# Gate tiles, activation buffers and accumulators in the expert stage of a hybrid decoder layer

## The chip, the cores and the metric

The kernel runs on one core of one Trainium2 chip. The metric is the time of one execution on the device in microseconds (us), taken as the median of several executions. TensorE is called PE here (PEld is its weight load), VectorE DVE, ScalarE ACT, GpSimd POOL, SyncE SP.

## The reference

One decoder layer over 1024 tokens (plus 16 meta tokens): a mixer (latent attention and retention, merged by gates), then a mixture of 16384 single-neuron experts. The change concerns the second part:

```python
def peer_sublayer(h, g_ffn, w_peer_q, keys_1, keys_2, peer_u, peer_v):
    x = rmsnorm(h, g_ffn).reshape(-1, shape[-1])
    q = (x @ w_peer_q).reshape(T, PEER_HEADS, PEER_DQ)
    ...
    eidx = (e1 * PEER_NKEYS + e2).reshape(T, PEER_HEADS * PEER_TOPK)
    gates = jax.nn.softmax(sc, axis=-1)
    ...
    def block(args):
        xt, it, gt = args
        act = jax.nn.gelu(jnp.einsum('td,tkd->tk', xt, peer_u[it]), approximate=False)
        return jnp.einsum('tk,tkd->td', gt * act, peer_v[it])
```

Each token has 128 chosen experts (8 heads of 16). For each it needs the dot product with a row of `peer_u`, a Gelu, the gate, and a weighted sum of rows of `peer_v`.

## The kernel before

The tokens are 8 blocks of 128. Three of them (group 0) take the **gathered** way: for each of the 128 chosen experts POOL fetches the 128 rows (one a token, 512 KB) by an indirect DMA, and DVE multiplies and sums (`gathered`, lines 1060 to 1091): first 128 steps with rows of `peer_u` against the normed tokens `xn`, then 128 steps with rows of `peer_v` added into two accumulators `acc`. At the start of a block `xn` and `acc[0]` are loaded and `acc[1]` is cleared; at its end the two are added and stored.

The other five blocks (640 tokens) take the **dense** way (`dense`, from line 1127): all 16384 experts are computed for all tokens, and a gate matrix that is zero for experts not chosen picks out what counts. The experts are 128 tiles of 128. Three steps belong to a tile: its scores (`scores`, line 1149: 48 matmuls into the buffers `tr`, then a Gelu by ACT into a tile `gl`), its weights (`weights`, line 1204: `gl` times the gates `gt` by DVE, then a split into `c_hi` by ACT and `c_lo` by DVE), and its part of the output (line 1239: matmuls of `c_hi` and `c_lo` with `peer_vt` into `zacc`). All products are made from a high and a low part of both factors in three matmuls (`mm3`, lines 246 to 248).

The dense part has two stages. In the **U stage** the scores of the first 48 tiles (AHEAD) are computed and stored to `gl_d`; meanwhile the routing of the last blocks and then the gate matrix (`gate_matrix`, 80 steps, stored to `gate_d` in 20 pieces) are made in the background. In the **V stage** the 128 tiles are taken in 16 groups of 8. The list `es` mixes quads of four stored tiles (their `gl` is loaded from `gl_d`, written L here) with quads of four tiles whose scores are computed now (C): the groups are CL, CL, CC, LC, and so on four times. In a group first come scores, loads and weights of its 8 tiles, then two passes (one for each half of the 1024 columns) of four pieces of `peer_vt` over 8 tiles, and after each pass five additions of `zacc` into `y` by DVE (line 1242). One gate tile `gt` holds the gates of four tiles, so each quad needs one; it is loaded in `weights` at a quad's first tile, into one buffer (GTB is 1). `gl` has three buffers, `c_hi` and `c_lo` eight, `raw` (a loaded piece of weights) three and its split parts three.

What sets the order around the change is a pacing by costs. Each piece that is split (`split_piece`, line 221) calls `pace` with `pacing["piece"]`, which is 6.5 in the dense part. `pace` gives each of two background queues that cost times a rate from RATES, and runs steps of the queue while its credit is positive: queue 0 the routing and gates (a gate step costs 1.7), queue 1 the gathered blocks (a row step costs 1.2). RATES[4] holds for the gate matrix, RATES[5] for the V stage. The rows of each engine are then put in order by the scheduler of the language, except for the row steps, which stay in the order of the program; SP issues all loads and stores but the gathered rows, in one queue.

Of the kernel before, what the change touches and what calls it, by code (L numbers as in the profile page):

```python
# [12 lines left out]
F32 = mybir.dt.float32  # L13
BF16 = mybir.dt.bfloat16
# [25 lines left out]
GE = 8  # L40
CB = 8
AHEAD = 48
RING = 3
ROWS = 4
SPLIT = 3
GTB = 1
DELAY = 8.0
# [3 lines left out]
LEAVE = ((6, 6, 3), (0, 1, 1))  # L51
RATES = ((0.0, 0.0), (0.5, 0.2), (0.3, 0.3), (0.8, 0.2), (0.8, 0.45), (0.0, 0.5))

# [90 lines left out]
def hybrid_layer(ctx: ExitStack, tc: tile.TileContext, out, a, dbg=None):  # L144
# [8 lines left out]
    dram = ctx.enter_context(tc.tile_pool(name="dram", bufs=1, space=DRAM))  # L153

    gat = ctx.enter_context(tc.tile_pool(name="gat", bufs=1, side="right"))

# [93 lines left out]
    def square_sum(src, acc):  # L250
        junk = work.tile([P, TW], F32, name="zt").bitcast(BF16)
        S.activation(junk[:, :src.shape[-1]], src, AF.Square, accum_out=acc)
# [63 lines left out]
    def group(g):  # L316
# [273 lines left out]
        def retention(hp):  # L590
# [45 lines left out]
            def add_state(i):  # L636
                pst = tr()
                for s in range(2):
                    T.matmul(pst[64 * s:64 * s + 64, 0:P], qn[:, i, 128 + 64 * s:128 + 64 * s + 64],
                             vr[:, i, P * s:P * s + P], start=True, stop=True)  # L640
                new = work.tile([P, P], F32, name=f"state{hp}")
                if hp in state:
                    V.tensor_tensor(new, pst[:, 0:P], state[hp], OP.add)
                else:
                    V.tensor_copy(new, pst[:, 0:P])
                state[hp] = new
# [179 lines left out]
        def merge():  # L826
            mg = own.mg
            for c in range(KD):
                for s, src in enumerate((own.oTs, own.yTs)):
# [6 lines left out]
                    for j, w in enumerate(split_pieces(a["w_ret" if s else "w_mla"][c], n, P)):  # L836
                        mm3(pz[:, 1, :W], w, src[j], j == 0, j == n - 1)
                        if j % 2:
                            yield
                    th = work.tile([P, TW], F32, name="zt")[:, :W]  # L840
                    S.activation(th, pz[:, 0, :W], AF.Tanh, scale=0.5)
# [218 lines left out]
    def gathered(b, eidx, gate):  # L1060
# [11 lines left out]
        nc.sync.dma_start(xn, xn_d[b])  # L1072
        acc = [gat.tile([P, D], F32, name=f"acc{s}", bufs=1) for s in range(2)]
        nc.sync.dma_start(acc[0], h2_d[b])
        V.memset(acc[1], 0.0)
        dots = work.tile([P, 128], F32, name="dots")
        for n in range(256):
            while todo and len(rows) < ROWS - 1:
# [4 lines left out]
            else:  # L1083
                if not k:
                    S.activation(dots, dots, AF.Gelu)
                    V.tensor_tensor(dots, dots, gate, OP.mult)
                op = V.scalar_tensor_tensor(acc[k % 2], row, dots[:, k:k + 1], acc[k % 2], op0=OP.mult, op1=OP.add)  # L1087
            tc.keep_in_program_order(op)
# [4 lines left out]

    def gate_matrix(i, kt, gT, p):

# [31 lines left out]
    def dense(xT):  # L1127
# [21 lines left out]
        def scores(e):  # L1149
            hi, lo = split_piece(1024, lambda r: nc.sync.dma_start(r, a["peer_ut"][e].rearrange("p c e -> p (c e)")))  # L1150
            gl = up.tile([P, DT], F32, name="gl", bufs=3)
            for n in order:
# [8 lines left out]
        def routes():  # L1161
# [12 lines left out]
            pacing["rates"] = RATES[4]  # L1174
            gms, gm = open_pool("gm")
            for i, (kt, gT) in enumerate(routed):
                yield from gate_matrix(i, kt, gT, gm)
            gms.close()
# [13 lines left out]
        for b in range(NGATH, NBLK):  # L1192
            ys.append(vp.tile([P, D], F32, name=f"y{b}"))
            nc.sync.dma_start(ys[-1], h2_d[b])
        gt = {}

        def activations(e):
            if e >= AHEAD:
                return scores(e)
            gl = up.tile([P, DT], F32, name="gl", bufs=3)  # L1200
            nc.sync.dma_start(gl, gl_d[e])
            return gl

        def weights(e, gl):

            if e % 4 == 0:
                gt[0] = vp.tile([P, nt, 4, TS], F32, name="gt", bufs=GTB)
                nc.sync.dma_start(gt[0], gate_d[:, :, TS * e:TS * e + 4 * TS].rearrange("n p (e t) -> p n e t", e=4))
            V.tensor_tensor(gl.rearrange("p (n t) -> p n t", t=TS), gt[0][:, :, e % 4],
                            gl.rearrange("p (n t) -> p n t", t=TS), OP.mult)  # L1210
# [5 lines left out]

        es = [4 * n + k for n in sorted(range(P // 4), key=lambda n: (n + 0.5) / AHEAD if 4 * n < AHEAD else
                                        (n + 0.5 - AHEAD / 4) / (P - AHEAD)) for k in range(4)]
        for e0 in range(0, P, GE):
            group = es[e0:e0 + GE]  # L1220
# [38 lines left out]
    V.tensor_scalar(g_gnh, g_gn, 0.5, None, op0=OP.mult)  # L1259
    mask_a = load_const("mask_a", a["c_mask_a"], [P, P])  # L1260
    mask_b, ident_b = (const.tile([P, P], BF16, name=n) for n in ("mask_b", "ident_b"))
    V.tensor_copy(mask_b, mask_a)
    V.tensor_copy(ident_b, ident)
    mask_r = load_const("mask_r", a["c_mask_r"], [P, P])
    iota = load_const("iota", a["c_iota"], [P, P])
    iota_i = const.tile([P, 16, 2 * H], BF16, name="iota_i")
    V.tensor_copy(iota_i, iota[:, 0:16].unsqueeze(2).to_broadcast([P, 16, 2 * H]))
    iota_2 = const.tile([P, P, 2], BF16, name="iota_2")
    V.tensor_copy(iota_2, iota.unsqueeze(2).to_broadcast([P, P, 2]))
    gqr = load_const("gqr", bcast(a["g_qk"], 32, 64), [P, 32])  # L1270
# [18 lines left out]
    for n, now in enumerate(groups):  # L1289
# [5 lines left out]
        interleave([now.merge()] + ([following.latents()] if following else []), STEPS[1][n])  # L1295
        rest = now.output()
    dense(rest)
    finish(1)

# [17 lines left out]
```

## Time and profile before

| what | us |
| --- | --- |
| median of three runs | 3574.49 (3563.3 to 3585.4) |
| the profiled execution | 3571.28 |
| its span, first to last instruction | 3569.5 |
| mixer and routing of the last group, about | 0 to 1420 |
| U stage, about | 1420 to 2003 |
| V stage, about | 2003 to 3560 |

The profile is of one execution. The profiled execution is within 0.1% of the median of the runs. Its span is 1.8 us shorter than its time. Busy times of PE overlap from one matmul to the next, so the step from one start to the next tells what a matmul takes, not its own duration.

### The profile page before, as it was taken

What the parts mean: (1) busy time and instruction counts of PE and PEld (TensorE: products, weight loads), DVE (VectorE), ACT (ScalarE), POOL (GpSimd) and SP (SyncE); (2) the same over time, 40 slices, a digit from 0 to 9 for tenths busy, and PEclk for the clock granted to TensorE, in tenths of its full rate; (3) what the DMA queues carried; (4) which work ended last, traced back from release to release, by engine and by line L of the source; (5) the groups of instructions that cost most, each with busy time, mean ns of one, the idle gap of its engine ahead of it and who ended that gap; (6) DMA issues with size and microseconds to landing.
All of it is one profiled execution on the core that took longest, in us unless ns stands there. A gap on an engine that the chain in (4) does not pass through costs nothing.

```text
span 3569.5 us, 53608 instructions
## 1 busy us (share of the span) xinstructions
PE 3322.8 (93%) x20376; PEld 3022.3 (85%) x20376; DVE 2687.7 (75%) x5659; ACT 1268.1 (36%) x2097; POOL 1090.4 (31%) x772
## 2 busy tenths in 40 slices
PE   8999989989789998999999799999999999999999
PEld 7888988788767898999999788888788778887788
DVE  5645469898796676798988578777778777877776
ACT  3445334544445533234566222222222222222221
POOL 0000000112011122013434445454445454554454
PEclk9999999999899999999999899999999999999999
DMA  3322353557654377456777888888889888988886
GB/s 129 121 78 94 133 193 113 167 201 253 215 156 139 135 239 254 152 177 238 284 289 295 305 289 305 306 308 301 287 284 321 288 291 290 322 307 288 286 300 246
DMA packets 329251, 837.12 MB, mean 235 GB/s; under 512 B 45713, under 2 KB 140689, under 8 KB 326177
## 3 DMA queue, kind: packets, MB, share of 16 engines
q1 hardware_dynamic: 218400, 431.00, 35.4%
q0 software_dynamic: 110592, 402.70, 32.0%
q8 instruction: 160, 2.62, 0.3%
q14 instruction: 99, 0.80, 0.1%
HBM read 755.16 MB, written 78.43 MB: 234 GB/s over the span
## 4 chain that ended last, share of the span: by engine, by line
PE 49%; issue 17%; DMA 13%; DVE 11%; POOL 6%; ACT 3%; POOLq 0%; SPq 0%; DVEq 0%; ACTq 0%
PE zacc L246 10%; PE zacc L248 10%; PE zacc L247 10%; DMA row<-in_peer_v_dram,eidx 7%; POOL row L1065 6%; PE tr L246 4%; PE tr L247 4%; PE tr L248 4%; DMA gt<-gate_d 3%; DVE wlo L219 2%; PE tr L765 2%; PE sc L729 1%; DVE acc L1087 1%; ACT whi L218 1%; DMA row<-in_peer_u_dram,eidx 1%
## 5 line engine op out<-in xcount | busy, mean ns | idle before, releaser
L1065 POOL DMA_INDIRECT row<-in_peer_u_dram,eidx x384 | 486.3, 1266 | 1731.5 <-DVE row L1082 839.9
L218 ACT ACTIVATE whi<-raw 128x1024 fp32r<-128x1024 f32 (+2 forms) x508 | 520.7, 1026 | 1274.3 <-PE zacc L248 643.5
L219 DVE TENSOR_TENSOR wlo<-raw,whi 128x1024 fp32r<-128x1024 f32 (+2 forms) x508 | 599.5, 1181 | 369.6 <-ACT whi L218 368.7
L1065 POOL DMA_INDIRECT row<-in_peer_v_dram,eidx x384 | 603.9, 1573 | 718.5 <-DVE acc L1087 605.4
L246 PE MATMUL zacc<-whi,c_hi 128*128 128x512 f32 x1280 | 509.1, 398 | 57.0 <-ACT c_hi L218 45.9
L1087 DVE SCALAR_TENSOR_TENSOR acc<-row,dots,acc 128x1024 f32<-128x1024 f32 x384 | 482.0, 1278 | 91.0 <-DMA row<-in_peer_v_dram,eidx 90.2
L248 PE MATMUL zacc<-whi,c_lo 128*128 128x512 f32 x1280 | 506.8, 396 | 2.9 <-DVE c_lo L219 2.9
L247 PE MATMUL zacc<-wlo,c_hi 128*128 128x512 f32 x1280 | 506.3, 396 | 0.0
L1082 DVE SCALAR_TENSOR_TENSOR row<-row,xn 128x1024 f32<-128x1024 f32 x384 | 463.2, 1218 | 54.7 <-DMA row<-in_peer_u_dram,eidx 54.3
L246 PE MATMUL tr<-xT_hi,whi 128*128 128x384 f32 (+1 forms) x1216 | 416.3, 342 | 40.5 <-ACT gl L1158 39.3
L247 PE MATMUL tr<-xT_lo,whi 128*128 128x384 f32 (+1 forms) x1216 | 411.9, 339 | 0.0
L248 PE MATMUL tr<-xT_hi,wlo 128*128 128x384 f32 (+1 forms) x1216 | 411.7, 339 | 0.0
L246 PEld LDWEIGHTS zacc<-whi,c_hi 128*128 128x128 f32 x1280 | 245.4, 192 | 115.2 <-ACT c_hi L218 49.3
L246 PE MATMUL tr<-x_hi,whi 128*128 128x256 f32 x1024 | 295.9, 289 | 12.7 <-ACT whi L218 10.2
L248 PEld LDWEIGHTS zacc<-whi,c_lo 128*128 128x128 f32 x1280 | 244.7, 191 | 60.0 <-DVE c_lo L219 8.6
L247 PE MATMUL tr<-x_lo,whi 128*128 128x256 f32 x1024 | 290.2, 283 | 0.0
L248 PE MATMUL tr<-x_hi,wlo 128*128 128x256 f32 x1024 | 290.1, 283 | 0.0
L247 PEld LDWEIGHTS zacc<-wlo,c_hi 128*128 128x128 f32 x1280 | 245.3, 192 | 50.7
L246 PEld LDWEIGHTS tr<-xT_hi,whi 128*128 128x128 f32 x1216 | 233.6, 192 | 43.2 <-ACT gl L1158 40.8
L246 PE MATMUL zacc<-whi,hn_hi 128*128 128x256 f32 x832 | 250.8, 301 | 3.8 <-ACT pT L780 1.3
L247 PE MATMUL zacc<-wlo,hn_hi 128*128 128x256 f32 x832 | 238.9, 287 | 1.4 <-DVE wlo L219 1.4
L248 PE MATMUL zacc<-whi,hn_lo 128*128 128x256 f32 x832 | 238.1, 286 | 0.0
(286 smaller groups left out, 6728.8 us busy)
## 6 DMA issues: line engine op xcount, KB each, us to landing
raw<-in_peer_ut_dram SPq DMA_DIRECT2D x128, 512.0 KB, 5.5
raw<-in_peer_vt_dram SPq DMA_DIRECT2D x128, 512.0 KB, 6.2
gate_d<-stage SPq DMA_DIRECT2D x20, 2048.0 KB, 9.1
gt<-gate_d SPq DMA_DIRECT2D x32, 1280.0 KB, 14.6
raw<-in_w_nat_dram SPq DMA_DIRECT2D x72, 512.0 KB, 3.5
raw<-in_w_z_dram SPq DMA_DIRECT2D x48, 512.0 KB, 3.3
gl_d<-gl SPq DMA_DIRECT2D x48, 320.0 KB, 2.9
gl<-gl_d SPq DMA_DIRECT2D x48, 320.0 KB, 6.4
```

The lines of the kernel that those rows point to most:

```text
L218: S.activation(hi, src, AF.Copy)
L219: V.tensor_tensor(lo, src, hi.bitcast(F32), OP.subtract)
L246: T.matmul(o, st[0], mv[0], start=first, stop=False)
L247: T.matmul(o, st[0], mv[1], start=False, stop=False)
L248: T.matmul(o, st[1], mv[0], start=False, stop=last)
L729: T.matmul(sc[:, c, 0:w], qh, kT[0:96, k0:k0 + w], start=True, stop=c < nch - 1)
L765: T.matmul(oo, vh[:, c + k], pT[:, k], start=False, stop=c + k == b)
L1065: G.indirect_dma_start(out=row, out_offset=None, in_=table, in_offset=bass.IndirectOffsetOnAxis(ap=eidx[:, k:k + 1], axis=0))
L1082: op = V.scalar_tensor_tensor(row, row, 1.0, xn, op0=OP.mult, op1=OP.mult, accum_out=dots[:, k:k + 1])
L1087: op = V.scalar_tensor_tensor(acc[k % 2], row, dots[:, k:k + 1], acc[k % 2], op0=OP.mult, op1=OP.add)
```

## The change

`gt` gets two buffers, and the tile of the next quad is loaded where the quad before it begins (the first before the first group). `gl` gets five buffers. RATES[4] goes from 0.8 to 0.9 for the gates, RATES[5] from 0.5 to 0.52 for the gathered rows. A gathered block waits for 6.0 of credit before its first row step. The second accumulator is no longer a buffer of its own: it takes the buffer of `xn` after the last step that reads `xn`, and its first step multiplies and does not add, so nothing is cleared. To make room, buffers that only the mixer needs (`zt`, the retention states, two masks and a bf16 identity) move to a pool `mw` that is closed before the dense part, and `iota_2` is made in the U stage, ahead of the gates.

```diff
+GLB = 5
-GTB = 1
+GTB = 2
-RATES = ((0.0, 0.0), (0.5, 0.2), (0.3, 0.3), (0.8, 0.2), (0.8, 0.45), (0.0, 0.5))
+RATES = ((0.0, 0.0), (0.5, 0.2), (0.3, 0.3), (0.8, 0.2), (0.9, 0.45), (0.0, 0.52))
...
+    mixers = ExitStack()
+    mw = mixers.enter_context(tc.tile_pool(name="mw", bufs=2))
...
-        junk = work.tile([P, TW], F32, name="zt").bitcast(BF16)
+        junk = mw.tile([P, TW], F32, name="zt").bitcast(BF16)
...
-                new = work.tile([P, P], F32, name=f"state{hp}")
+                new = mw.tile([P, P], F32, name=f"state{hp}")
...
-        acc = [gat.tile([P, D], F32, name=f"acc{s}", bufs=1) for s in range(2)]
+        acc = [gat.tile([P, D], F32, name="acc", bufs=1)]
         nc.sync.dma_start(acc[0], h2_d[b])
-        V.memset(acc[1], 0.0)
         dots = work.tile([P, 128], F32, name="dots")
+        yield 6.0
...
-                op = V.scalar_tensor_tensor(acc[k % 2], row, dots[:, k:k + 1], acc[k % 2], op0=OP.mult, op1=OP.add)
+                if k == 1:
+                    acc.append(gat.tile([P, D], F32, name="xn", bufs=1))
+                    op = V.tensor_scalar(acc[1], row, dots[:, k:k + 1], None, op0=OP.mult)
+                else:
+                    op = V.scalar_tensor_tensor(acc[k % 2], row, dots[:, k:k + 1], acc[k % 2], op0=OP.mult, op1=OP.add)
...
-            gl = up.tile([P, DT], F32, name="gl", bufs=3)
+            gl = up.tile([P, DT], F32, name="gl", bufs=GLB)
...
+            iota_2 = gm.tile([P, P, 2], BF16, name="iota_2")
+            V.tensor_copy(iota_2, iota.unsqueeze(2).to_broadcast([P, P, 2]))
...
-        gt = {}
+        gts = deque()
+
+        def gate_tile(e):
+            gts.append(vp.tile([P, nt, 4, TS], F32, name="gt", bufs=GTB))
+            nc.sync.dma_start(gts[-1], gate_d[:, :, TS * e:TS * e + 4 * TS].rearrange("n p (e t) -> p n e t", e=4))
...
             if e % 4 == 0:
-                gt[0] = vp.tile([P, nt, 4, TS], F32, name="gt", bufs=GTB)
-                nc.sync.dma_start(gt[0], gate_d[:, :, TS * e:TS * e + 4 * TS].rearrange("n p (e t) -> p n e t", e=4))
-            V.tensor_tensor(gl.rearrange("p (n t) -> p n t", t=TS), gt[0][:, :, e % 4],
+                if e != es[0]:
+                    gts.popleft()
+                if e != es[-4]:
+                    gate_tile(es[es.index(e) + 4])
+            V.tensor_tensor(gl.rearrange("p (n t) -> p n t", t=TS), gts[0][:, :, e % 4],
...
+        gate_tile(es[0])
         for e0 in range(0, P, GE):
...
+    mixers.close()
     dense(rest)
```

**SP at the start of the V stage.** In the rows below `y` is the output, `gt` a gate tile, `gl<-gl_d` the load of a stored tile's scores, `raw<-in_peer_ut_dram` a piece for scores and `raw<-in_peer_vt_dram` one for the output. Before:

```order
L1194 DMA y_21061<-h_d 128x1024
L1208 DMA gt<-gate_d 128x20x128
L1232 DMA raw<-in_peer_vt_dram 128x1024 x4
L1201 DMA gl<-gl_d 128x640 x2
L1232 DMA raw<-in_peer_vt_dram 128x1024
L1208 DMA gt<-gate_d 128x20x128
L1201 DMA gl<-gl_d 128x640
L1232 DMA raw<-in_peer_vt_dram 128x1024
L1201 DMA gl<-gl_d 128x640
L1232 DMA raw<-in_peer_vt_dram 128x1024
L1208 DMA gt<-gate_d 128x20x128
```

and now:

```order
L1208 DMA gt<-gate_d 128x20x128
L1194 DMA gl_d<-gl 128x640
L1157 DMA raw<-in_peer_ut_dram 128x1024
L1208 DMA gt<-gate_d 128x20x128
L1157 DMA raw<-in_peer_ut_dram 128x1024
L1194 DMA gl_d<-gl 128x640
L1157 DMA raw<-in_peer_ut_dram 128x1024
L1248 DMA raw<-in_peer_vt_dram 128x1024
L1194 DMA gl_d<-gl 128x640
L1248 DMA raw<-in_peer_vt_dram 128x1024 x4
L1214 DMA gl<-gl_d 128x640 x4
L1208 DMA gt<-gate_d 128x20x128 x2
```

The second `gt` used to stand behind the pieces of the first group's output and its first two stored tiles; now it stands three rows behind the first, ahead of two pieces for the last computed scores of the first group, and the two `gt` of the second group are together, ahead of three pieces of the first group's second pass. The stored tiles are loaded four at a time.

**DVE in the second half of a CL group.** This is the fifth group, from the last computed tiles of the C quad (`gl<-gt` is the multiplication by the gates, `c_lo` and `wlo` are low parts, `row,dots<-row,xn` a row step of a gathered block). Before:

```order
L1209 TENSOR_TENSOR gl<-gt,gl 128x640
L1082 SCALAR_TENSOR_TENSOR row,dots<-row,xn 128x1024
L219 TENSOR_TENSOR c_lo<-gl,c_hi 128x640
L1082 SCALAR_TENSOR_TENSOR row,dots<-row,xn 128x1024
L219 TENSOR_TENSOR wlo<-raw,whi 128x1024
L1082 SCALAR_TENSOR_TENSOR row,dots<-row,xn 128x1024
L1209 TENSOR_TENSOR gl<-gt,gl 128x640 x3
L219 TENSOR_TENSOR c_lo<-gl,c_hi 128x640 x3
L1082 SCALAR_TENSOR_TENSOR row,dots<-row,xn 128x1024 x2
L1209 TENSOR_TENSOR gl<-gt,gl 128x640
L219 TENSOR_TENSOR wlo<-raw,whi 128x1024
L219 TENSOR_TENSOR c_lo<-gl,c_hi 128x640
```

and now:

```order
L1224 TENSOR_TENSOR gl<-gt,gl 128x640
L1085 SCALAR_TENSOR_TENSOR row,dots<-row,xn 128x1024
L222 TENSOR_TENSOR c_lo<-gl,c_hi 128x640
L1085 SCALAR_TENSOR_TENSOR row,dots<-row,xn 128x1024 x2
L1224 TENSOR_TENSOR gl<-gt,gl 128x640 x5
L222 TENSOR_TENSOR c_lo<-gl,c_hi 128x640 x5
L222 TENSOR_TENSOR wlo<-raw,whi 128x1024
L1085 SCALAR_TENSOR_TENSOR row,dots<-row,xn 128x1024 x3
L222 TENSOR_TENSOR wlo<-raw,whi 128x1024
```

Before, the four stored tiles were multiplied in two goes (three and one), behind the split of the next `peer_vt` piece (`wlo`). Now the multiplications of the last computed tile and of all four stored tiles stand together, with their five `c_lo` behind them, and the split of the piece comes after these ten rows.

## Rows read from the trace of the kernel before

**Rows 1.** The page, part 1: busy time, share of the span, instructions.

```profile
PE 3322.8 (93%) x20376; PEld 3022.3 (85%) x20376; DVE 2687.7 (75%) x5659; ACT 1268.1 (36%) x2097; POOL 1090.4 (31%) x772
```

**Rows 2.** Windows: stretch, length, busy PE, PEld, DVE, ACT, POOL, clock, DMA, GB/s.

```profile
1700.00:1900.00 200.00, 200.00 (x1508) 199.59 (x1508) 178.52 (x198) 121.32 (x142) 91.91 (x38) 1.00 0.78 291
...
2003.00:3560.00 1557.00, 1455.55 (x7549) 1286.18 (x7548) 1191.90 (x1435) 362.60 (x491) 757.96 (x551) 0.96 0.85 295
2300.00:2400.00 100.00, 100.00 (x525) 88.46 (x524) 80.78 (x120) 21.65 (x28) 51.88 (x41) 1.00 0.91 318
...
2700.00:2800.00 100.00, 99.94 (x547) 89.80 (x546) 82.23 (x81) 23.54 (x32) 51.01 (x40) 1.00 0.89 314
3100.00:3200.00 100.00, 100.00 (x555) 90.44 (x555) 81.28 (x118) 25.32 (x37) 52.92 (x41) 1.00 0.87 301
```

**Rows 3.** Waits, 2003 to 3560: engine and line, releaser, us, times, longest.

```profile
DVE gl L1209 <- DMA gt<-gate_d: 107.4, 17, 9.5
DVE acc L1087 <- DMA row<-in_peer_v_dram,eidx: 66.9, 40, 5.7
...
PE zacc L246 <- ACT c_hi L218: 45.9, 8, 7.6
...
PE tr L246 <- ACT gl L1158: 41.4, 6, 20.1
...
PE zacc L246 <- DVE y L1242: 9.9, 10, 2.1
```

**Rows 4.** Timeline of three engines around one late gate tile (fifth group).

```profile
2426.08 0.37 SPq L1208 DMA_DIRECT2D gt<-gate_d  x1
...
2441.66 2.30 DVE L1209 TENSOR_TENSOR gl<-gt,gl 128x640 f32<-128x640 f32 x3 [8.19 <-DMA gt<-gate_d]
...
2443.31 0.79 PE L246 MATMUL zacc<-whi,c_hi 128*128 128x512 f32 x1 [6.53 <-ACT c_hi L218]
```

**Rows 5.** DMA issues by name: KB each, median us from issue to landing.

```profile
gt<-gate_d SPq DMA_DIRECT2D x32, 1280.0 KB, 14.6
...
xn<-xn_d SPq DMA_DIRECT2D x3, 512.0 KB, 4.4
```

**Rows 6.** Matmuls by line, 2003 to 3560: count, busy, mean ns, idle before.

```profile
L246 PE MATMUL zacc<-whi,c_hi 128*128 128x512 f32 x1276 | 507.5, 398 | 57.0 <-ACT c_hi L218 45.9 <-DVE y L1242 9.9 <-ACT whi L218 1.2
...
L246 PE MATMUL tr<-xT_hi,whi 128*128 128x384 f32 x624 | 215.5, 345 | 39.1 <-ACT gl L1158 39.0
...
L246 PE MATMUL tr<-x_hi,whi 128*128 128x256 f32 x617 | 174.3, 282 | 2.6 <-ACT gl L1158 2.4
```

**Rows 7.** Timeline of PE, 2003 to 2041: start, duration, instruction.

```profile
2003.00 0.28 PE L248 MATMUL tr<-x_hi,wlo 128*128 128x256 f32 x1
2023.34 0.69 PE L246 MATMUL tr<-xT_hi,whi 128*128 128x384 f32 x1 [20.06 <-ACT gl L1158]
...
2024.46 0.52 PE L246 MATMUL tr<-xT_hi,whi 128*128 128x384 f32 x1
2024.78 0.52 PE L247 MATMUL tr<-xT_lo,whi 128*128 128x384 f32 x1
...
2029.61 0.28 PE L246 MATMUL tr<-x_hi,whi 128*128 128x256 f32 x1
...
2032.46 0.34 PE L246 MATMUL tr<-xT_hi,whi 128*128 128x384 f32 x1
...
2036.63 0.39 PE L246 MATMUL zacc<-whi,c_hi 128*128 128x512 f32 x1
...
2040.52 0.39 PE L248 MATMUL zacc<-whi,c_lo 128*128 128x512 f32 x1
```

**Rows 8.** Groups by line, 1700 to 1900: the gate steps on DVE and PE.

```profile
L1120 DVE TENSOR_TENSOR ob<-eq,gT 128x1024 f32<-128x1024 bf16 x48 | 58.4, 1218 | 1.2 <-PE zacc L1105 1.2
L219 DVE TENSOR_TENSOR wlo<-raw,whi 128x1024 fp32r<-128x1024 f32 x17 | 20.8, 1224 | 19.8 <-ACT whi L218 19.8
...
L1105 PE MATMUL zacc<-ob,oa 128*128 128x128 f32 x754 | 95.5, 281 | 0.0
```

**Rows 9.** Waits of the SP queue for gate tiles, 2003 to 3560.

```profile
SPq L1208 <- DVE gl L1209: 50.4, 31, 5.5
```

More of the change, by code (lines that the diff above doesn't have):

```diff
@@ L839, in merge @@
                             yield
-                    th = work.tile([P, TW], F32, name="zt")[:, :W]
+                    th = mw.tile([P, TW], F32, name="zt")[:, :W]
                     S.activation(th, pz[:, 0, :W], AF.Tanh, scale=0.5)
@@ L1091, in gathered, with gate_matrix @@
         nc.sync.dma_start(out[P * b:P * b + P], acc[0])
-    def gate_matrix(i, kt, gT, p):
+    def gate_matrix(i, kt, gT, iota_2, p):
         stage = {}
@@ L1175, in routes @@
             gms, gm = open_pool("gm")
+            iota_2 = gm.tile([P, P, 2], BF16, name="iota_2")
+            V.tensor_copy(iota_2, iota.unsqueeze(2).to_broadcast([P, P, 2]))
             for i, (kt, gT) in enumerate(routed):
-                yield from gate_matrix(i, kt, gT, gm)
+                yield from gate_matrix(i, kt, gT, iota_2, gm)
             gms.close()
@@ L1199, in activations @@
                 return scores(e)
-            gl = up.tile([P, DT], F32, name="gl", bufs=3)
+            gl = up.tile([P, DT], F32, name="gl", bufs=GLB)
             nc.sync.dma_start(gl, gl_d[e])
@@ L1259, in hybrid_layer @@
     V.tensor_scalar(g_gnh, g_gn, 0.5, None, op0=OP.mult)
-    mask_a = load_const("mask_a", a["c_mask_a"], [P, P])
-    mask_b, ident_b = (const.tile([P, P], BF16, name=n) for n in ("mask_b", "ident_b"))
+    mask_a, mask_r = (mw.tile([P, P], F32, name=n, bufs=1) for n in ("mask_a", "mask_r"))
+    nc.sync.dma_start(mask_a, a["c_mask_a"])
+    mask_b, ident_b = (mw.tile([P, P], BF16, name=n, bufs=1) for n in ("mask_b", "ident_b"))
     V.tensor_copy(mask_b, mask_a)
     V.tensor_copy(ident_b, ident)
-    mask_r = load_const("mask_r", a["c_mask_r"], [P, P])
+    nc.sync.dma_start(mask_r, a["c_mask_r"])
     iota = load_const("iota", a["c_iota"], [P, P])
@@ L1267, in hybrid_layer @@
     V.tensor_copy(iota_i, iota[:, 0:16].unsqueeze(2).to_broadcast([P, 16, 2 * H]))
-    iota_2 = const.tile([P, P, 2], BF16, name="iota_2")
-    V.tensor_copy(iota_2, iota.unsqueeze(2).to_broadcast([P, P, 2]))
     gqr = load_const("gqr", bcast(a["g_qk"], 32, 64), [P, 32])
```

## The prediction

> **What bounds the kernel now.** I read the page first, then the windows by stage, then the waits of the V stage, then the timeline around one wait. The page says that PE is busy for 93% of the span [rows 1], so whatever gives time must do it where PE stands still or runs slowly. The windows show where: from 1700 to 1900, in the U stage, PE is busy for all 200 us at a granted clock of 1.00; from 2003 to 3560, in the V stage, it is busy for 1455.55 of 1557 us, at a clock of 0.96 [rows 2]. So 101.5 us are idle there.
>
> The waits name the reasons [rows 3]: PE waits 45.9 us in 8 goes for `c_hi`, 41.4 us in 6 goes for the Gelu's buffers `gl`, and 9.9 us for the additions into `y`. The first two are not the last link. DVE itself waits 107.4 us in 17 goes for `gt`, and one case shows the chain [rows 4]: the load of `gt` is issued at 2426.08, DVE gets it at 2441.66 (8.19 us idle), and PE begins again at 2443.31 after 6.53 us. A load takes 14.6 us to land [rows 5], and with one buffer it can't be issued before the last tile of the quad before has been multiplied. The 8 waits for `c_hi` are as many as there are CL groups (8 of 16): there the stored quad comes second, and PE has no scores to do meanwhile. The waits for `gl` belong to the first group (20.06 us [rows 7]) and to four CC groups, where the computed tiles run out of their three buffers behind a DVE that stands; a sixth of 2.4 us is of the other segment [rows 6] and not clearly of this kind.
>
> An idle stretch costs more than itself. After the 20 us the 384-column matmuls follow each other at 0.32 us (2024.46, 2024.78), later at 0.174 us (24 steps from 2032.46 to 2036.63) [rows 7]: about half, as between the levels of 1.2 and 2.4 GHz. How much that is in the stage comes from counting. Steps at full clock are 0.174 us (384 columns), 0.119 us (256 columns, 24 steps from 2029.61 to 2032.46) and 0.229 us (512 columns, 17 steps from 2036.63 to 2040.52) [rows 7]. The stage needs 3 x 624 of the first, 3 x 617 of the second [rows 6] and 3840 of the third (the program's 1280 in each of three lines; the trace lacks a few): 326 + 220 + 879 = 1425 us. The stage takes 1557, so 132 us are lost, 101.5 idle and 31 in slow steps.
>
> **The change part by part.**
>
> *Gate tiles.* With two buffers the load of a quad's gates is issued at the first multiplication of the quad before. In a CL group that is some three tiles of scores ahead of its first use, and eight pairs of steps (8 x (0.174 + 0.119) x 3 = 7.0 us) make a tile, so 21 us against 14.6. In the order of SP the two tiles of a whole group even stand together, a group ahead. All of DVE's waits for `gt` should go, and with them PE's for `c_hi` (45.9) and for `gl` but for the 2.4 us: 39.0. That is 85 us. The slow steps go with the idle time that made them: 31 x 85 / 101.5 = 26 us. Together 111 us. The wait that is next late on PE is the one for `y`, 9.9 us, which stays.
>
> *Five `gl`.* These let the four stored tiles be loaded at once and PE run two tiles further ahead of DVE. With gates in time nothing waits for that, so I count nothing; if gates came late all the same, the stalls of the four CC groups (41.4 - 20.06 - 2.4 = 18.9 us) would be covered by those two tiles, 14 us a group.
>
> *Gates sooner (0.8 to 0.9).* From 1700 to 1900 there are 17 pieces and 48 gate steps, 2.8 a piece [rows 8]; now 3.15. A step is 16 matmuls at 95.5 / 754 = 0.127 us and on DVE at most 3.7 us (one row of 1.218 and two smaller ones for `eq`, which I bound by the same). So a piece gets 0.7 us longer on PE (11.8 to 12.5 us) and at most 1.3 us on DVE (10.5, as DVE is busy 178.5 of 200 us [rows 2], to 11.8). DVE stays below PE. The number of steps is the same, so the U stage keeps its length: 0, with 8 us more as the upper bound, if DVE becomes the slower one for the 25 pieces that then have gates (0.3 us each). It is what hides the first `gt`: the gates end before the last tiles of the stage, and the 20.06 us above depend on it.
>
> *Gathered rows (0.5 to 0.52, and 6.0 at a block's start).* The number of rows is the same; three more units of 6.0 against 4% more a piece. They end a little sooner before the last `y`, not on the path. Cost 0.
>
> *Shared accumulator.* Three clears go and three steps change their kind, all on DVE, each below 1.3 us: 0. But `xn` of the next block can be loaded only after the last addition, and the first row step waits for it on DVE with the next additions into `y` queued behind. The load takes 4.4 us [rows 5]; at the first of the two changes of block one row stands between, at the second six. It costs from 0 to 5 us each; I take 3, the nearest to the first case, 6 in all.
>
> *The lump.* In CL groups ten DVE rows now stand ahead of the split of the third `peer_vt` piece. Five multiplications and five `c_lo` come to some 8 us (three `gl` rows took 2.30 us [rows 4]), with 1.2 for the split; PE needs that piece two pieces after its last scores, 2 x 30 x 0.229 = 13.7 us. It fits, with 4 us to spare, unless a gathered row is late: those waits are up to 5.7 us [rows 3]. From 0 to 2 us in each of 8 groups, and as much for the other stretches that get tighter: I take 10 in all, bounds 0 and 35.
>
> *Moves of masks, states and `iota_2`.* The same loads, one small copy later. 0, within 4 either way.
>
> The sum: 3571.3 (the profiled execution) - 111 + 6 + 10 = 3476. The median of the runs lies 3.2 us above that execution: 3479. By the bounds the likeliest case runs from 3452 (all 132 us but 9.9 for `y`, nothing added) to 3519 (111 gained, 10 for `xn`, 35 for the lump, 8 in the U stage, 3 for the moves).
>
> **The rivals.**
>
> *The transfers become the bound.* The stage moves 295 GB/s x 1557 us = 459 MB, and if it shortens to 1557 - 95 = 1462 us it needs 314 GB/s in the mean. Three of its stretches of 100 us have PE busy throughout, at 318, 314 and 301 GB/s, 311 in the mean [rows 2]. For: the DMA engines are at 0.87 to 0.91 there, and DVE's waits for rows grow with it. Against: PE lost nothing at those rates, and DVE was busy for only 80 to 82%. If 301, the lowest of the three, is what holds over the stage: 459 / 0.301 = 1525 us, 32 less than now, 3543.
>
> The Trainium skill, page DMA: Bandwidth & Descriptors, section Where 436 GB/s comes from, puts the limit of the HBM side at about 358 GB/s a core. No stretch here comes to that (318 at most); by it the stage could not be shorter than 459 / 0.358 = 1282 us, which bounds nothing, and the sum would stay as it is.
>
> *It doesn't do what it says.* The tile of the stored quad could still land late, because SP issues it behind pieces that wait for their buffers. Then the 45.9 us and their share of the slow steps (14) stay, and only 39 + 12 go: 3571 - 51 + 16 + 3 = 3539. Against: in the new order both gates of the second group stand ahead of three pieces of the first.
>
> *SP stands in front of the pieces* (the one that ends slower). A `gt` issue waits for a multiplication by DVE and everything behind it on SP waits too, now with the stored tiles' last multiplication as the condition and pieces of `peer_vt` behind. Today such waits are 50.4 us in 31 goes, 5.5 at most [rows 9]. Three raw pieces lead by 3 x 6.9 = 20.6 us, less the landing (no more than 14.6, the gate tile's). So from 6 us of standing PE would stop. To eat the 111 us a group of 16 would have to lose 7, a standing of 13 us in each; at 18 us the kernel ends at 3571 - 111 + 16 x 12 + 3 = 3655. Against: a longest wait of 5.5 us, and multiplications that no longer wait for gates.
>
> **How the numbers follow.** The forecast 0.82; transfers as the bound 0.06; late gates as before 0.08; SP in front 0.04. About 1% (36 us) is what a measurement of this kernel tells from no change, so faster means below 3539. The forecast lies below that by its own range, the second and third rivals around the mark: half of each counts as faster, half as no change, which gives 0.82 + 0.07 = 0.89 and 0.07; slower 0.04. The range from 3446 to 3530 leaves out the slower rival, most of the other two and a little of the forecast on both sides, under 2 in 10.
>
> **What would show it.** Right: DVE's wait for `gt` falls from 107 us to under 10; PE's waits for `c_hi` and `gl` in the V stage together from 87 us to under 15; the granted clock there rises from 0.96 to 0.99; the V stage is some 95 us shorter at 311 GB/s or more; the U stage is as long as now within 8 us. Wrong: PE waits for `c_hi` or `whi` at the same groups, with DVE's waits for rows grown (transfers), with `gt` still named (late gates), or with SP held at line 1208 for over 6 us (SP in front); or DVE stands for `xn` more than 5 us twice.

## The result and the profile after

The changed kernel takes **3529.82 us** (median of 4 runs, 3529.13 to 3532.09) against 3573.11 us for the kernel before on the same chip: ratio 0.9878, 95% interval 0.9847 to 0.9909. So it is faster by 43 us, less than half of the forecast 95, and by luck just inside the forecast range (3446 to 3530). One execution of a_rows5_glb3 below took 3675.49 us at a granted clock of 0.84 and stands outside its ratio. The page after, part 1, answers to [rows 1]:

```profile
PE 3303.4 (94%) x20376; PEld 3008.2 (85%) x20376; DVE 2683.7 (76%) x5656; ACT 1263.2 (36%) x2097; POOL 1082.6 (31%) x772
```

The windows after (stretch, length, busy PE, PEld, DVE, ACT, POOL, clock, DMA share, GB/s) answer to [rows 2]:

```profile
1700.00:1900.00 200.00, 200.00 (x1514) 199.58 (x1514) 181.22 (x204) 124.59 (x146) 87.65 (x36) 1.00 0.80 295
2003.00:3520.00 1517.00, 1446.15 (x7550) 1279.62 (x7549) 1186.68 (x1431) 355.89 (x486) 754.38 (x552) 0.98 0.87 301
2300.00:2400.00 100.00, 99.05 (x547) 89.29 (x546) 79.25 (x117) 23.89 (x34) 52.40 (x40) 1.00 0.86 299
2700.00:2800.00 100.00, 95.00 (x488) 83.05 (x487) 76.77 (x75) 24.23 (x34) 53.78 (x39) 1.00 0.88 307
3100.00:3200.00 100.00, 96.00 (x489) 83.32 (x487) 77.96 (x102) 23.85 (x32) 46.45 (x37) 1.00 0.90 309
```

PE is still idle for 70.9 of 1517 us (101.5 of 1557 before), and its clock rose from 0.96 to 0.98. Two of the three stretches that had next to no idle PE before have 4 to 5 us now. The waits of the V stage after (2003 to 3520: who waits for whom, us, times, longest) answer to [rows 3]:

```profile
DVE gl L1224 <- DMA gl<-gl_d: 56.4, 34, 4.6
DVE row L1085 <- DMA row<-in_peer_u_dram,eidx: 50.3, 42, 4.4
DVE acc L1094 <- DMA row<-in_peer_v_dram,eidx: 46.0, 27, 4.3
DVE xn L1094 <- DMA row<-in_peer_v_dram,eidx: 29.5, 30, 3.6
...
DVE row L1085 <- DMA xn<-xn_d: 10.4, 2, 7.3
...
PE zacc L249 <- DVE y L1258: 53.9, 15, 8.1
PE zacc L251 <- DVE c_lo L222: 11.4, 7, 2.7
PE tr L249 <- ACT gl L1165: 3.1, 2, 2.2
PE zacc L249 <- ACT c_hi L221: 1.4, 1, 1.4
```

DVE's 107.4 us for `gt` are gone, and with them PE's for `c_hi`. In their place PE waits 53.9 us for the additions into `y` (9.9 before), and DVE waits 56.4 us for stored activations (3.1 before). The timelines of SP, of DVE and of PE around the wait that ends at 2529.48 show what stands ahead of a late `y`:

```profile
2489.55 2.84 SPq L1214 DMA_DIRECT2D gl<-gl_d  x4
2499.47 5.33 SPq L1208 DMA_DIRECT2D gt<-gate_d  x2
```

```profile
2515.25 1.28 DVE L1094 SCALAR_TENSOR_TENSOR xn<-row,dots,xn 128x1024 f32<-128x1024 f32 x1 [1.56 <-DMA row<-in_peer_v_dram,eidx]
2516.45 1.22 DVE L222 TENSOR_TENSOR wlo<-raw,whi 128x1024 fp32r<-128x1024 f32 x1
2520.36 1.28 DVE L1094 SCALAR_TENSOR_TENSOR acc<-row,dots,acc 128x1024 f32<-128x1024 f32 x1 [2.69 <-DMA row<-in_peer_v_dram,eidx]
2522.79 1.28 DVE L1094 SCALAR_TENSOR_TENSOR xn<-row,dots,xn 128x1024 f32<-128x1024 f32 x1 [1.15 <-DMA row<-in_peer_v_dram,eidx]
2524.52 1.28 DVE L1094 SCALAR_TENSOR_TENSOR acc<-row,dots,acc 128x1024 f32<-128x1024 f32 x1 [0.44 <-DMA row<-in_peer_v_dram,eidx]
...
2528.05 1.28 DVE L1258 TENSOR_TENSOR y<-zacc,y 128x512 f32<-128x512 f32 x2
```

```profile
2529.48 0.77 PE L249 MATMUL zacc<-whi,c_hi 128*128 128x512 f32 x1 [6.84 <-DVE y L1258]
```

Four loads of stored tiles and two gate tiles are issued within some 15 us; behind them gathered rows land late, DVE takes them in order, and the additions into `y` stand behind them; PE begins again after 6.84 us. The case is a common one: added up from the trace, in the 25 us ahead of PE's ten waits for `y` of over 1 us (51.1 us together) DVE waited 51.2 us for rows, 7.3 for `xn` and only 2.4 for stored activations.

**Where the 42 us of the two profiled executions came from.** I cut both by two marks, the first score matmul and the first and last matmul into `zacc` of the V stage. Up to the first score: 1429.6 before, 1422.8 after (-6.8; the change only moves a few small buffers here, and the length in the kernels below lies between 1410 and 1432). First score to first `zacc`: 607.1, 590.1 (-17.0), of which 8.3 is PE's last long wait ahead of the V stage, called the border below, 20.06 before and 11.77 after. First to last `zacc`, called V below: 1526.5, 1508.0 (-18.5). The tail is 6.4 in both. So the V stage, where most of the 95 us were to go, gave 18.5.

### The profile page after: what moved, and what is told of

Its sections match the earlier page's. It is cut to its first block, busy times and chain, and to the rows that moved or that the text cites. A ratio compares the mean times of both kernels' runs of the same rounds, so it can differ in the third digit from the quotient of the medians.

```text
span 3527.3 us, 53571 instructions
## 1 busy us (share of the span) xinstructions
PE 3303.4 (94%) x20376; PEld 3008.2 (85%) x20376; DVE 2683.7 (76%) x5656; ACT 1263.2 (36%) x2097; POOL 1082.6 (31%) x772
## 4 chain that ended last, share of the span: by engine, by line
PE 37%; issue 27%; POOL 12%; DVE 11%; DMA 10%; ACT 2%; POOLq 0%; SPq 0%; DVEq 0%; ACTq 0%
POOL row L1068 12%; PE zacc L249 8%; DMA row<-in_peer_v_dram,eidx 7%; PE zacc L251 7%; PE zacc L250 7%; DVE wlo L222 2%; PE tr L249 2%; PE tr L250 2%; PE tr L251 2%; PE tr L768 2%; PE sc L732 1%; DVE row L1085 1%; DMA row<-in_peer_u_dram,eidx 1%; PE sc L778 1%; PE tr L766 1%
## 5 line engine op out<-in xcount | busy, mean ns | idle before, releaser
L1068 POOL DMA_INDIRECT row<-in_peer_v_dram,eidx x384 | 597.8, 1557 | 643.9 <-DVE acc L1094 262.3
L249 PE MATMUL zacc<-whi,c_hi 128*128 128x512 f32 x1280 | 510.0, 398 | 56.4 <-DVE y L1258 53.9
L251 PE MATMUL zacc<-whi,c_lo 128*128 128x512 f32 x1280 | 508.2, 397 | 11.4 <-DVE c_lo L222 11.4
L1094 DVE SCALAR_TENSOR_TENSOR acc<-row,dots,acc 128x1024 f32<-128x1024 f32 x192 | 245.7, 1280 | 50.5 <-DMA row<-in_peer_v_dram,eidx 50.2
L1094 DVE SCALAR_TENSOR_TENSOR xn<-row,dots,xn 128x1024 f32<-128x1024 f32 x189 | 241.6, 1279 | 41.8 <-DMA row<-in_peer_v_dram,eidx 41.8
```

What stands on the lines that cost most here:

```text
L249: T.matmul(o, st[0], mv[0], start=first, stop=False)
L251: T.matmul(o, st[1], mv[0], start=False, stop=last)
L1068: G.indirect_dma_start(out=row, out_offset=None, in_=table, in_offset=bass.IndirectOffsetOnAxis(ap=eidx[:, k:k + 1], axis=0))
```

## The experiments

V is the time from the first to the last `zacc` matmul of the profiled execution. The last four columns are waits within it: PE's for `y`, and DVE's for rows, for stored activations and for gate tiles. Executions of one kernel differ by up to 27 us (a_rate50), so a few us of V, which is read from one execution, say little. Times are medians, or the single run (the kernel before, run beside each, took 3562 to 3573 us); ratios to it, with their intervals, stand in the text.

| kernel | time | V | PE y | DVE rows | gl_d | gt |
|---|---|---|---|---|---|---|
| before | 3573.1 | 1526.5 | 9.9 | 117.0 | 3.1 | 98.3 |
| after | 3529.8 | 1508.0 | 53.9 | 127.5 | 56.4 | 0 |
| a_glb4, 4 `gl` | 3540.2 | 1514.2 | 67.6 | 118.6 | 58.3 | 0 |
| a_glb3, 3 `gl` | 3524.2 | 1498.2 | 59.3 | 127.1 | 66.6 | 0 |
| a_rows5_glb4 | 3510.6 | 1474.3 | 37.8 | 42.8 | 63.3 | 0 |
| a_rows5_glb3 | 3493.7 | 1461.5 | 32.7 | 32.2 | 75.0 | 0 |
| a_rows3 | 3686.5 | 1654.1 | 127.2 | 393.4 | 19.5 | 0 |
| a_nogather | 3399.7 | 1404.5 | 0 | 0 | 34.8 | 0 |
| b_nogather | 3405.1 | 1409.8 | 0 | 0 | 6.3 | 33.3 |
| a_half | 3490.0 | 1467.8 | 40.5 | 187.9 | 51.6 | 0 |
| a_halfbytes | 3421.8 | 1413.3 | 4.6 | 95.0 | 31.4 | 0 |
| b_acc_r5 | 3553.3 | 1521.4 | 12.9 | 26.1 | 2.3 | 118.2 |

**Is it the order on DVE (five `gl`), or the rows?** Edits: `GLB = 5` to 3 or 4, `ROWS = 4` to 5.

a_glb3: 

> The changed kernel with three activation buffers instead of five (all else as changed). In the changed kernel four loads of stored activations are issued together, VectorE stands on the five multiplications that they feed (56.4 us of waits for the stored activations) and comes late to the rows and to the y additions (TensorE then waits 53.9 us for those). Theory LUMP (the five buffers put all that in one stretch): with three buffers the waits for stored activations fall from 56 to under 20 us, TensorE's wait for y from 54 to under 25 us, time 3490 to 3510 us. Theory ROWS (rows land late whatever the order, four row buffers): VectorE's waits for rows stay near 97 us and TensorE's wait for y stays 40 to 60 us, time 3530 +- 8 us.

a_glb4: 

> The changed kernel with four activation buffers instead of five. LUMP: about half of the effect of three buffers, waits for stored activations 25 to 40 us, time 3510 to 3525 us. ROWS: y wait 40 to 60 us, time 3530 +- 8 us.

a_rows5_glb4: 

> Four activation buffers and five row buffers instead of four (five activation buffers leave no room for a fifth row buffer), to be read against the run with four activation buffers. ROWS: one more row in flight while VectorE is late, TensorE's wait for y halves, and the time is 20 to 30 us under that run's. LUMP: VectorE's order is what makes it late, the time is within 8 us of that run's.

Measured: three buffers 0.9878 (0.9853 to 0.9903), four 0.9916 (0.9894 to 0.9938), four with a fifth row buffer 0.9833 (0.9813 to 0.9853). With three buffers DVE's wait for stored activations is longer (66.6) and PE's for `y` no shorter: LUMP falls. DVE's wait for rows stays (127.1; the 97 of the expectation leaves out the 29.5 of `xn<-row`). That four are slower than both three and five follows no line; the intervals touch, and I read up to 10 us as what any new order of the instructions can do. The fifth row buffer takes 30 us from the run with four `gl`, as ROWS has it.

**What are the rows worth, with and without the change?**

```diff
-                    background[1].append(gathered(blocks[i], *found))
+                    pass
```

a_nogather: 

> The changed kernel without its gathered blocks: no row is gathered, and nothing is added to the accumulators (that part of the computation is left out). ROWS: TensorE's wait for y falls under 5 us, and the time from the first to the last zacc matmul from 1508 to about 1430 us, time near 3450 us. LUMP without rows: VectorE still stands on the stored activations, y wait over 25 us and time over 3480 us.

b_nogather: 

> The kernel before without its gathered blocks (that part of the computation is left out), to be read against the changed kernel without them (3399.71 us; 1404.5 us from the first to the last zacc matmul; no wait of TensorE in the V stage). If the prediction's term for the gate tiles (85 us idle and 26 us of slow steps) was right and the gathered rows ate the gain: VectorE still waits some 100 us for the gate tile, and the time from the first to the last zacc matmul is 1480 to 1515 us, 75 to 110 more than without those waits. If the gate tiles were worth little by themselves: under 1450 us.

Measured: without rows the two kernels differ by 5 us. The changed one takes 3399.7 us where ROWS had about 3450, and its V is 1404.5 where ROWS had about 1430. The windows of both, 1988 to 3392, and DVE's wait for gate tiles in the kernel before without rows:

```profile
1988.00:3392.00 1404.00, 1404.00 (x7486) 1253.88 (x7485) 541.05 (x611) 352.65 (x480) 0.00 (x0) 1.00 0.36 114
```

```profile
1988.00:3392.00 1404.00, 1401.16 (x7464) 1248.77 (x7463) 542.78 (x607) 356.26 (x480) 0.00 (x0) 1.00 0.37 115
...
DVE gl L1209 <- DMA gt<-gate_d: 33.3, 16, 3.3
...
PE zacc L248 <- DVE c_lo L219: 1.8, 4, 0.7
```

PE is never idle in the first and 2.8 us in the second, at a clock of 1.00: this is the V stage at full speed. If the price of the gate tiles was right, they were to cost 75 to 110 us here; they cost 5. Without rows one buffer is no bound: DVE waits 33.3 us for its tiles, but has so much time (it is busy for 39%) that PE hardly notices. And DVE's waits for gates and stored activations come to 39.6 us there and to 34.8 without the late gates: standing for the one, DVE finds the other landed, which fits the 56.4 us of `gl_d` that came up when the gates were in time. The gates' load lands in 8.1 us instead of 14.6 [rows 5], as the issues of b_nogather (KB each, median us to landing) show:

```profile
raw<-in_peer_vt_dram SPq DMA_DIRECT2D x128, 512.0 KB, 3.5
...
gt<-gate_d SPq DMA_DIRECT2D x32, 1280.0 KB, 8.1
...
gl<-gl_d SPq DMA_DIRECT2D x48, 320.0 KB, 4.1
```

The rows, with their transfers and DVE's work on them, cost the V stage 1526.5 - 1409.8 = 117 us before and 1508.0 - 1404.5 = 103 us after. The change has little to give where they bind. The border is in time without rows too: PE has no wait of over 3 us there in either kernel.

**DVE's work on the rows, or their transfers?** The first edit halves the work and leaves the transfers, the second halves both, the third takes a buffer away (`ROWS = 3`).

```diff
-                op = V.scalar_tensor_tensor(row, row, 1.0, xn, ...
+                op = V.scalar_tensor_tensor(row[:, :512], row[:, :512], 1.0, xn[:, :512], ...
...
-            G.indirect_dma_start(out=row, out_offset=None, in_=table,
+            G.indirect_dma_start(out=row[:, :512], out_offset=None, in_=table.rearrange("r (h c) -> (r h) c", h=2),
```

a_half: 

> The changed kernel, in which VectorE multiplies and adds only the first 512 of a gathered row's 1024 numbers (the other half of that part of the computation is left out); every row is still gathered whole, into the same four buffers, and all other transfers stay. VECTOR ORDER (VectorE's work in order, 1178 us busy and 194 us of waits for transfers in the 1508 us of the V stage, is what TensorE waits for): the row work halves (some 335 us less), TensorE's waits for y and c_lo fall from 65 to under 10 us, first to last zacc matmul 1405 to 1430 us, time 3400 to 3445 us. TRANSFERS (rows land late whatever VectorE does): y wait over 35 us and more than 1470 us from first to last zacc matmul.

a_halfbytes: 

> The changed kernel gathering rows of 512 instead of 1024 numbers (the others are left out of that part of the computation, and the rows are those of other experts), with VectorE multiplying and adding 512, to be read against the run that gathers whole rows and works on half of them (1467.8 us from first to last zacc matmul, 40.5 us of waits for y). BYTES (the rows come late because they and the other transfers fill the engines): the waits for y fall under 10 us, first to last zacc matmul under 1425 us. ROUND TRIP (a row takes its time whatever it carries, and four buffers are few): y wait over 25 us and over 1445 us.

a_rows3: 

> The changed kernel with three row buffers instead of four. ROUND TRIP or BYTES alike: the buffers limit how many rows are under way; from five to four buffers cost 30 us, from four to three costs more, 60 to 150 us: time 3590 to 3680 us, TensorE's wait for y over 100 us. If the rows are not the bound of the V stage: under 3550 us.

Windows and waits of a_half:

```profile
2014.00:3482.00 1468.00, 1423.98 (x7490) 1262.51 (x7488) 896.21 (x1422) 352.82 (x482) 599.44 (x548) 0.99 0.90 309
...
PE zacc L249 <- DVE y L1258: 40.5, 12, 5.6
...
DVE row L1085 <- DMA row<-in_peer_u_dram,eidx: 88.2, 67, 5.8
DVE acc L1094 <- DMA row<-in_peer_v_dram,eidx: 55.0, 35, 6.9
...
DVE xn L1094 <- DMA row<-in_peer_v_dram,eidx: 44.7, 35, 5.6
```

of a_halfbytes:

```profile
2000.00:3414.00 1414.00, 1409.38 (x7491) 1254.90 (x7490) 889.27 (x1424) 353.14 (x482) 594.72 (x548) 1.00 0.70 218
...
PE zacc L249 <- DVE y L1259: 4.6, 5, 2.0
```

and of a_rows3:

```profile
2024.00:3678.00 1654.00, 1468.02 (x7489) 1288.47 (x7488) 1186.44 (x1428) 349.76 (x484) 726.38 (x551) 0.95 0.82 275
...
PE zacc L249 <- DVE y L1258: 127.2, 16, 13.5
PE tr L249 <- ACT gl L1165: 41.9, 24, 4.2
```

With half the work DVE is busy for 896 instead of 1178 us, yet V shortens by only 40 and PE still waits 40.5 us for `y`: DVE now waits 188 us for rows. VECTOR ORDER falls, though DVE's work has its part (40 of the 103 us); of its rival's numbers the `y` wait fits, and V misses by 2 us. With half the bytes as well V is 1413, 9 us over full speed, at a DMA share of 0.70 instead of 0.90. So rows are late by their bytes, together with the other transfers (the other half of the work is left out in both); a row lands in 3.8 or 3.9 us there (median, `peer_u` and `peer_v`), against 6.2 and 7.0 in the kernel before. The ring of row buffers decides how much of that DVE sees: from three to four to five buffers V is 1654, 1508 or 1514, and 1474, at 275, 301 or 299, and 307 GB/s. a_rows3 came out 6 us slower than the range expected.

**The gate tiles' part of the load, and the rate of the rows.** a_nogt loads two gate tiles and uses them in turn; a_rate50 puts the last number of `RATES` back.

a_nogt: 

> The changed kernel with only its first two gate tiles loaded and used in turn (30 of 32 loads of gate tiles are left out, so the gates of most experts are those of others). BURST (the gate tiles, now two back to back, hold up the rows): the waits of VectorE for rows fall from 126 us to under 60, TensorE's wait for y from 54 to under 20 us, time 3470 to 3490 us. ROUND TRIP (four row buffers over a row's way, whatever else is loaded): y wait stays over 35 us, time over 3500 us.

a_rate50: 

> The changed kernel with the rows' rate of the V stage at 0.50 as before, instead of 0.52. RATE (4% more rows a piece are what is too much): TensorE's wait for y falls from 54 to under 35 us; as the last row then comes some 50 us later (it came 39 us ahead of the last zacc matmul), the end is at best where it was, 3515 to 3530 us. ROUND TRIP: y wait 45 to 55 us, time 3525 to 3540 us.

a_nogt took 3511.74 us: V 1486.3, DVE's waits for rows 73.9, PE's for `y` 40.6 us, as ROUND TRIP has it. Thirty tiles fewer help the rows, but take only 22 us from V. a_rate50 took 0.9915 (0.9894 to 0.9935), 3535.29 us, as ROUND TRIP has it. Its profiled execution is the slowest of the four (3553.75): PE's wait for `y` 49.5 us, V 8 us shorter, but the last row was issued at 3539 us, 18 us after the last matmul, and the rows ran on alone.

**Does the kernel before have the same bound?** Shared accumulator alone, and the fifth row buffer that it makes room for:

b_acc_r5: 

> The kernel before with the shared accumulator alone taken from the change, and five row buffers in the space that it frees; one gate tile, three activation buffers and the rates as before. ROUND TRIP (the rows' way through few buffers binds, in the kernel before too): 25 to 45 us under the kernel before, 3525 to 3545 us, though the gate tile is late as before (waits of VectorE for it over 70 us). GATE (the one gate tile binds in the kernel before): within 12 us of the kernel before.

```profile
2025.00:3547.00 1522.00, 1438.99 (x7492) 1272.68 (x7490) 1169.69 (x1419) 356.96 (x482) 743.80 (x543) 0.97 0.86 297
...
PE zacc L246 <- ACT c_hi L218: 48.5, 8, 7.6
PE tr L246 <- ACT gl L1161: 19.2, 5, 5.2
...
DVE gl L1212 <- DMA gt<-gate_d: 118.2, 16, 9.2
```

0.9946 (0.9929 to 0.9963), 17 us, between both theories; V gave 5 of them, and most of the rest lies between first score and first `zacc` (594.0 against 607.1). Here rows land nearly in time (26.1 us of waits), and the gate tiles hold PE as in [rows 3]: V is 1521.4. So with rows moving there are **two bounds close together**. Loosening the rows alone takes 5 us from V, the gates alone 12 to 28 (four, five and three `gl`), both together (a_rows5_glb4, a_rows5_glb3) 52 and 65. Put otherwise: b_acc_r5 and a_rows5_glb3 both have five row buffers and three `gl`, and between them the second gate buffer and the rest of the change take 60 us from V (1521.4 to 1461.5), where it took 5 without rows and, with four row buffers, 18.5 (28 with three `gl`).

**The smaller terms.** a_sep_glb4 gives the second accumulator its own buffer again, a_u80 puts the gates' rate back to 0.8.

a_sep_glb4: 

> The changed kernel with four activation buffers and the second accumulator in a buffer of its own, so that xn of the next block is loaded ahead, to be read against the run with four activation buffers and the shared buffer (3540.18 us, VectorE waits 13.2 us for xn). If the sharing costs what the prediction says (6 us): VectorE's wait for xn goes to 0 and the time is 3528 to 3538 us. If the wait costs nothing since VectorE stands at the rows instead: 3540 +- 5 us.

a_u80: 

> The changed kernel with the gates' rate of the U stage at 0.8 as before, instead of 0.9. If the sooner gates are what shortens the stretch from the first score to the first zacc matmul (607 us before, 590 with the change): it is 600 us or more, and the time 3538 to 3550 us. If not: 590 +- 4 us and 3530 +- 8 us.

a_sep_glb4 took 3529.56 us, 0.9899 (0.9876 to 0.9922): the 13.2 us for `xn` are gone, and V is 1497.8 against 1514.2. The sharing comes to 11 us by the medians and 6 by the ratios; the intervals of the two overlap, so neither is firm. a_u80 took 0.9916 (0.9883 to 0.9948): first score to first `zacc` 595.3 us, the wait at the border 17.74. That is between both theories, and the time, 3533.31 us, is that of the second. The other kernels with the sooner gates and whole rows lie between 589 and 597 us there, with waits of up to 19.78 at the border, and b_acc_r5, with the rate of before, has 594.0. So no gain of the sooner gates is shown. What the 17 us come from is not settled: 8.3 are the border, and the kernel before also stood 6.16 us at 1696.55, which the changed kernel doesn't; why was not tried.

**Towards a faster kernel.** a_rows5_glb3 combines three `gl` with five rows; the others vary it, or (a_gs33) the changed kernel: the rows' rate 0.51, stored tiles in a ring of their own, gate tiles issued by ScalarE.

a_rows5_glb3: 

> Five row buffers and three activation buffers, to be read against five and four (3510.58 us) and against four and three (3524.22 us). ROUND TRIP: the fifth row buffer brings 15 to 30 us here too, so 3494 to 3509 us. LUMP (the stored tiles together): three activation buffers bring 10 us or more over four here too (3490 to 3500 us); otherwise within 6 us of 3510 us.

a_r5_g3_r51: 

> Five row buffers, three activation buffers (3493.68 us) and the rows' rate of the V stage at 0.51 instead of 0.52. The last row then comes some 25 us later (it was issued 43 us ahead of the last zacc matmul), still ahead of the end; fewer rows a piece, so TensorE's wait for y (32.7 us) falls by up to 10 us. Time 3483 to 3493 us; if the rate does nothing, 3494 +- 6 us.

a_gs33: 

> The changed kernel with two rings, three buffers for the computed and three for the stored activations, so that the loads of stored ones do not wait for computed ones to be multiplied. If the waits for stored activations (56.4 us, new in the changed kernel, in the place of the waits for the gate tile) are a part of what makes VectorE late: they fall under 20 us, and the V stage shortens by as much or more, time 3480 to 3505 us. If VectorE only stands elsewhere instead (at the rows): gl_d waits fall, those for rows grow by as much, time 3525 +- 8 us.

a_r5_gs22: 

> Five row buffers, and two rings of two buffers each for computed and stored activations, to be read against five row buffers and one ring of three (3493.68 us). If both waits of VectorE add up: waits for stored activations from 75 to under 40 us, time 3465 to 3485 us. If the smaller ring for computed tiles costs TensorE as much in waits for gl: 3490 us or more.

a_r5_g3_gtact: 

> Five row buffers, three activation buffers, and the gate tiles' loads issued by ScalarE instead of SyncE. In the changed kernels SyncE's issue behind the first gate tile stands for 10 to 20 us, the raw pieces behind it come late, and TensorE stands 11.8 to 17.4 us at the first computed tile of the V stage. If that is the issue behind the tile of small pieces: the 17.4 us fall under 5 and the time from 3493.68 to 3475 to 3485 us. If the transfers themselves are late: the stall stays over 10 us and the time within 6 us.

a_rows5_glb3 took **3493.68 us, 0.98 (0.978 to 0.9819)** and a_r5_g3_r51 3494.75 us, 0.9784 (0.9757 to 0.9811): equal, and the fastest here. The V stage of a_rows5_glb3:

```profile
2026.00:3487.00 1461.00, 1422.27 (x7486) 1261.43 (x7486) 1174.10 (x1423) 353.80 (x482) 745.95 (x547) 0.99 0.89 310
```

It lies 30 us under a_glb3, as ROUND TRIP has it, but also 17 us under a_rows5_glb4, as LUMP has it. Three `gl` are 16 and 17 us faster than four in both pairs, though DVE waits longer for stored activations with three; why is not shown. 57 us over full speed are left. In the 25 us ahead of its nine waits for `y` of over 1 us (32.5 us) DVE waited 17.4 us for stored activations and 16.7 for rows, so the stored activations may be the next to look at.

The other three are misses. Own rings: 3551.12 us (0.995, 0.9932 to 0.9968) and 3545.51 us (0.993, 0.9907 to 0.9953); stored tiles are now issued between the two gate tiles of most CL groups, and in a_gs33 DVE waits 36.7 us for gates again beside 49.7 for stored activations. Whether those waits cost PE anything by themselves stays open. Gate tiles by ScalarE: 3533.86 us (0.9895, 0.9877 to 0.9913), 40 us more than with SyncE (34 by the ratios); DVE then waits 119.2 us for stored activations, and the stall at the border is 13.88 us. The Trainium skill, page DMA: Bandwidth & Descriptors, section Issuing engines are not separate DMA queues, says that DMAs share the same engines whoever starts them; this run agrees in so far as nothing was gained.

## Why the prediction was wrong

*Right.* The gate tiles were late, and a second buffer mends that: DVE's wait for `gt` went from 107 us to 0 (forecast under 10), PE's for `c_hi` from 45.9 to 1.4. The direction is right, and the clock rose, to 0.98 instead of 0.99.

*The step that failed* is the sentence that closes the term of the gate tiles: "The wait that is next late on PE is the one for `y`, 9.9 us, which stays." It did not stay: it became 53.9, with `c_lo` 11.4. The 85 us were taken as free because their last link had gone. But while DVE stood for a gate tile, rows went on landing: behind each of its 15 waits of over 2 us in the kernel before, the next three row instructions begin without a wait. When it no longer stands there, it comes to the rows before they do, and to the stored activations: in V 98 us of waits for gates went, but 53 for stored activations, 10 for rows and 10 for `xn` came, so that its waits for transfers fell only from 218 to 194 us. Ahead of PE's waits for `y` it is the rows that DVE waits for. The tests are b_nogather, where the same single gate buffer costs 5 us without rows, and the fifth row buffer, with which the change takes 60 us from V. So the -111 was mis-sized, at -18.5 in V and -8.3 at the border. Had the next bound been sized by the rows, the loss of V against full speed (1526.5 - 1404.5 = 122 us) would have been shared between both.

*Gathered rows, "Cost 0"* fails in the same way. The number of rows is the same, but they were the second bound. The rate of 0.52 is not the culprit (a_rate50: V 8 us shorter at 0.50, the end no sooner).

*Transfers become the bound* was nearly the true case and had a chance of 0.06. Its figure, 301 GB/s over the stage, is the one measured, but by chance: 301 is no limit of the transfers. With five row buffers the stage moves 307 to 311, with four and half of DVE's work on the rows (a_half) 309, and the page of the kernel before has a slice of 89 us at 322, above the 318 that the prediction took for the most. Against the rival I had held that PE lost nothing at 318 GB/s and that DVE was busy for only 80 to 82%. The first was true of stretches of 100 us, in which DVE did wait 11.0, 9.9 and 6.5 us for rows; it does not carry over to the stage. The second counts no waits: over V before, DVE was busy for 1174.9 and waited 218 us for transfers, 1393 of 1526.5 us. (The other 132 are waits for ACT and PE; these are no sign of a full engine, as they are 825 us in b_nogather.)

*The lump* (+10): not shown; three `gl` undo the lump and the waits stay. *Shared accumulator* (+6): 6 to 11 by a_sep_glb4, not firm; 10.4 us of it seen as DVE's wait for `xn`, the longest 7.3 where I had bounded one at 5. *Gates sooner* (0): no gain shown. *Late gates* and *SP in front of the pieces* did not happen as drawn; but SP stands behind the issue of a gate tile (below), in the kernel before too, which the waits of [rows 9] don't hold and I had not priced.

## What to carry to other kernels

A wait that ends last is worth its length only if nothing else is nearly as late. Before a stall is counted as gain, take the next resource out altogether (here the gathered rows) in both versions, which shows what the stall is worth without it; then loosen it by a little (here one buffer), as a resource that is taken out takes its load on the others along. And for an engine that works in order, count its waits for transfers beside its busy time; 80% busy said nothing of its slack.

## What the runs showed of the hardware

With rows moving beside them, the loads of the kernel before take 1.6 to 1.8 times as long to land as in b_nogather (raw piece 6.2 against 3.5 us, stored activations 6.4 against 4.1, gate tile 14.6 against 8.1), at a DMA share of 0.85 [rows 2, 5]. The issues of the kernel before:

```profile
raw<-in_peer_vt_dram SPq DMA_DIRECT2D x128, 512.0 KB, 6.2
...
gl<-gl_d SPq DMA_DIRECT2D x48, 320.0 KB, 6.4
```

The issue that follows a gate tile's on its queue can stand. In the kernel before the 32 such issues on SP take 3.9 us in the median, in the changed kernel 2.0; the other 856 of each take 0.33, and no more than two of them over 1.5. The longest stand at the border of U and V. SP in the kernel before:

```profile
1994.39 0.42 SPq L1208 DMA_DIRECT2D gt<-gate_d  x1
1996.68 18.13 SPq L1232 DMA_DIRECT2D raw<-in_peer_vt_dram  x1
```

and in the changed kernel:

```profile
1951.29 0.42 SPq L1208 DMA_DIRECT2D gt<-gate_d  x1
1957.44 10.25 SPq L1194 DMA_DIRECT2D gl_d<-gl  x1
1967.79 0.38 SPq L1157 DMA_DIRECT2D raw<-in_peer_ut_dram  x1
1968.22 0.65 SPq L1208 DMA_DIRECT2D gt<-gate_d  x1
1968.96 10.04 SPq L1157 DMA_DIRECT2D raw<-in_peer_ut_dram  x1
```

The issue of a store, else 0.3 us, takes 10.25, the raw piece behind it comes late, and PE stands 11.77 us at 1977.75. In a_rows5_glb3 and a_rows5_glb4 the same issue took 19.8 and 20.1 us, and PE's stall was 17.4; in a_nogather it took 1.6. In a_nogt, which loads two gate tiles, the two issues behind them take 11.2 and 9.3 us, and no other of the V stage over 1.5. Where ScalarE issues the gate tiles (a_r5_g3_gtact), SP's issues at the border take 0.3 us, and the stand is on ScalarE, with the Gelu that PE waits for behind it:

```profile
1944.90 0.38 ACTq L1208 DMA_DIRECT2D gt<-gate_d  x1
...
1945.36 18.13 ACTq L1208 DMA_DIRECT2D gt<-gate_d  x1
1963.54 0.77 ACT L1165 ACTIVATE gl<-tr 128x384 f32<-128x384 f32 x2 [17.82 <-issue]
```

So the stand goes with the gate tile and not with SP. What in the load of a gate tile makes the next issue stand was not tried.
